# A two-layer decoder trunk on one core: last two row blocks and final norm by halves of the tokens, one mask product for two score blocks, new hand-over times

## The chip, the cores and the metric

The kernel runs on one core of a Trainium2 chip. The metric is the device time of one execution in microseconds (us); lower is better. The number for a kernel is the median over its runs.

## The reference: what is computed

Input is x, 512 tokens of 1024 features, in float32; the output has the same shape. Two layers follow each other, and a final norm ends the trunk. Each layer does:

```
hn = rms_norm(h);  p = hn @ W_in              # 1024 -> 2592, three groups of columns
yA = rwkv7(p[A])       # 4 heads of 64: a recurrence with a 64 x 64 state per head, then group norm and gate
yB = retention(p[B])   # 4 heads of 64: decaying linear attention in chunks of 128, then norm and gate
yC = latent_attention(p[C])  # 8 heads: scores of 96 features, causal softmax, values of 64
h  = h + concat(yA, yB, yC) @ W_out
h  = h + (silu(g) * u) @ W_down,  g, u = rms_norm(h) @ W_gate_up    # 1024 -> 2 x 2816 -> 1024
```

and in the end `out = rms_norm(h)`, with a learned factor per feature (`final_norm`). In the causal softmax a block of 128 queries, number ib = 0 to 3, sees (ib + 1) x 128 keys, and the last 128 of these are masked above the diagonal.

## The kernel before, in words

Features lie on the 128 partitions and the 512 tokens along the free axis, so h is eight tiles of 128 x 512. Wide products run with operands split into a high and a low part: `gemm` (L492) makes for each 128 x 128 weight tile three products, high x high, high x low and low x high. All products go through `mm` (L241, the instruction is L243) and all transposes through `tr` (L249); both pin the order of TensorE to the order of the program text. The other engines' order is chosen by the tile framework, unless an instruction is pinned in the same way.

Weights come from HBM in blocks. `fetch` loads one (L387), `convert` (L397 on) forms the high part on ScalarE (L403) and the low part by a subtraction (L404) on VectorE, or on POOL if the block's number stands in `POOL_LO`. `wnext` hands out the next block and keeps three ahead. A layer has 102 blocks: 0 to 10 time mixing and retention, 11 to 13 values, 14 to 20 gate and latents, 21 and 22 keys and values, 23 rotary queries, 24 and 25 queries, 26 to 33 the output product, then the feed-forward. The second layer's numbers begin at 102.

The order of the work is made by a small driver when the program is written out. One generator, `dense` (L1050 on), issues the wide products; others issue the time mixing (`rwkv`, `chain`, `group_norm`), the retention (`retnet`), the attention (`head`, `attend`), the key rotation and the sums of the feed-forward stage. The driver has a clock that advances by the estimated TensorE time of each product. A generator that hands over gives a delay from the table `T` (us, one dictionary per layer) or a condition; the driver then takes the generator that is due and stands first in priority (`p_...` of the same table; `dense` has 9, the last). So `T` sets where on TensorE each small piece stands between wide products. `EN` names the engine (d VectorE, p POOL, a ScalarE) of single instructions: key e542 multiplies two 128 x 512 tiles in `rwkv` (L660), key e757 adds two in `group_norm` (L881); both are on POOL. Each occurs twice in a layer.

`head` (L956 on) works one attention head. For ib = 3, 2, 1, 0 it takes a score tile in PSUM, multiplies queries and keys, adds the mask by a product of the identity with a table of 0 and -1e30, takes the row maximum on VectorE (L970), the exponential with its sum on ScalarE (L972), the reciprocal (L974) and the scaling (L975; POOL for ib = 2). The probabilities are then transposed, and `attend` multiplies them with the values when both heads of a pair are there. The query tiles are written by L1281 from a product and the factor of a norm, and the inverse roots of norms take two VectorE steps (L340, L341) with two operands in SBUF. The output product of a layer starts when the group norm's and the retention's four tiles (`mix` 0 to 3) are there; the last one hands over with the delay `group_norm3` before its last step.

In the feed-forward stage most gate and up products run over 256 tokens at a time, through sums of weight quarters and token halves (many of them on tiles of PSUM pool pd), and the down products between them over 512 (pool pm). The last step of a layer is eight row blocks of the remaining down product, each six weight tiles by three products of 512 columns; each block is added to h (L1418). In the second layer the square of a block is summed over blocks (L326, L327), and the block is scaled by `final_norm` (L1424). After the eighth block its square (L1428), a product with ones that sums over partitions (tile pm from acc and r), the inverse root by halves of the tokens (L1439 to L1443), eight products (L1446) and eight output DMAs on two queues (L1447) follow.

## Time and profile before

| | us |
|---|---|
| median of 3 runs | 1319.48 |
| lowest and highest | 1317.63, 1320.84 |
| the profiled execution, its own time | 1318.88 |
| its span, first to last instruction | 1317.1 |

The span is what a trace shows; the time also holds what lies around it, here 1.8 us. The profiled execution is 0.6 us faster than the median. In rows of the trace, PE is TensorE's products and PEld its weight loads, DVE is VectorE, ACT ScalarE, POOL GpSimd, SP the queue of the sync engine. Products are pipelined: the length of one overlaps the start of the next, so the cost of a product in a stream is the distance between starts. A product of float32 operands that is not split appears as two instructions.

### The profile page before, as it was taken

The numbers are of one execution on the slowest core, as the hardware profiler recorded it, in microseconds if no ns is written. First come the engines' busy times: TensorE is split into PE (matmuls) and PEld (weight loads), VectorE is DVE, ScalarE is ACT, GpSimd is POOL, SyncE is SP. The second block draws the span as 40 slices with busy tenths as digits, with TensorE's granted clock in tenths as the row PEclk, the third lists the DMA queues.
The fourth block names the chain that finished last, engine by engine and source line by source line (L and its number), as shares of the span: only waits on it lengthen the run. The fifth ranks groups of instructions, "written<-read, shape, count | busy, mean of one in ns | idle before, by whom it ended". The sixth has DMA issues, their size and how long they took to land. (4 is left out here: it accounts for less than half of the span.)

```text
span 1317.1 us, 20150 instructions
## 1 busy us (share of the span) xinstructions
PE 1274.7 (97%) x7774; PEld 1092.8 (83%) x7774; DVE 987.9 (75%) x1665; ACT 679.0 (52%) x1267; POOL 93.0 (7%) x82
## 2 busy tenths in 40 slices
PE   7999999899999999999999999989999999999996
PEld 5778787578899999999877887856888999999994
DVE  7797877747997777777667697686579877777774
ACT  7834456726454444545475345465355544444453
POOL 1130012200000000000012300121000000000000
PEclk9899999899999999999999899979999999999998
DMA  7434422223233333333522423131232333222231
GB/s 247 135 99 135 99 63 67 81 65 112 77 102 110 96 97 102 108 97 105 184 88 84 120 89 85 44 101 60 86 97 79 113 100 109 97 97 97 86 107 64
DMA packets 67512, 131.11 MB, mean 100 GB/s; under 512 B 29172, under 2 KB 33940, under 8 KB 67416
## 3 DMA queue, kind: packets, MB, share of 16 engines
q1 hardware_dynamic: 66040, 128.20, 31.4%
q8 instruction: 61, 1.00, 0.3%
q10 hardware_dynamic: 1232, 1.09, 0.2%
q0 software_dynamic: 144, 0.52, 0.1%
q14 instruction: 35, 0.29, 0.1%
HBM read 117.47 MB, written 9.18 MB: 96 GB/s over the span
## 5 line engine op out<-in xcount | busy, mean ns | idle before, releaser
L243 PE MATMUL pd<-u,wh 128*128 128x256 f32 (+1 forms) x3112 | 755.8, 335 | 8.4 <-ACT wh L403 5.9
L243 PEld LDWEIGHTS pd<-u,wh 128*128 128x128 f32 x3112 | 528.3, 191 | 71.6 <-issue 7.4
L243 PE MATMUL pd<-u,wl 128*128 128x256 f32 (+1 forms) x1556 | 516.9, 332 | 0.6 <-DVE wl L422 0.5
L243 PEld LDWEIGHTS pd<-u,wl 128*128 128x128 f32 x1556 | 296.9, 191 | 29.5 <-POOL wl L404 0.9
L243 PE MATMUL pm<-u,wh 128*128 128x512 f32 (+1 forms) x800 | 212.0, 352 | 0.0
L403 ACT CAST wh<-wr 128x1024 fp32r<-128x1024 f32 (+3 forms) x102 | 98.9, 974 | 167.8 <-PE pd L243 105.2
L243 PEld LDWEIGHTS pm<-u,wh 128*128 128x128 f32 x800 | 139.0, 190 | 18.3 <-DVE u L298 0.3
L404 DVE TENSOR_TENSOR wl<-wr,wh 128x1024 fp32r<-128x1024 f32 (+3 forms) x93 | 109.2, 1177 | 45.2 <-ACT wh L403 44.8
L243 PE MATMUL pm<-u,wl 128*128 128x512 f32 (+1 forms) x400 | 140.4, 351 | 0.0
L421 ACT CAST wh<-r 128x512 fp32r<-128x512 f32 x144 | 87.3, 618 | 98.9 <-PE pm L243 51.4
L421 ACT CAST wh<-wr 128x512 fp32r<-128x512 f32 x108 | 67.0, 620 | 78.6 <-PE pm L243 54.3
L422 DVE TENSOR_TENSOR wl<-r,wh 128x512 fp32r<-128x512 f32 x144 | 97.6, 687 | 8.7 <-ACT wh L421 6.5
L422 DVE TENSOR_TENSOR wl<-wr,wh 128x512 fp32r<-128x512 f32 x108 | 74.3, 689 | 24.4 <-ACT wh L421 22.3
L243 PEld LDWEIGHTS pm<-u,wl 128*128 128x128 f32 x400 | 75.7, 189 | 10.1
L1377 DVE TENSOR_TENSOR u<-u,pm 128x512 f32<-128x512 f32 x64 | 43.8, 684 | 43.9 <-PE pm L243 43.9
L243 PE MATMUL pm<-u,u 32*32 32x32 f32 (+4 forms) x728 | 68.4, 280 | 5.3 <-DVE u L742 4.0
L243 PEld LDWEIGHTS pm<-u,u 32*32 32x32 f32 (+3 forms) x728 | 51.9, 159 | 21.5 <-issue 14.0
L403 ACT CAST wh<-gg 128x1024 fp32r<-128x1024 f32 x32 | 33.6, 1049 | 42.0 <-issue 27.7
L243 PE MATMUL pd<-u,u 96*128 96x512 f32 (+3 forms) x128 | 50.9, 507 | 3.9 <-DVE u L1281 2.9
L404 POOL TENSOR_TENSOR wl<-wr,wh 128x1024 fp32r<-128x1024 f32 (+2 forms) x9 | 18.9, 2100 | 491.4 <-ACT wh L403 491.4
L432 DVE TENSOR_TENSOR r<-r,wr 128x512 f32<-128x512 f32 x72 | 49.5, 687 | 0.6
L404 DVE TENSOR_TENSOR wl<-gg,wh 128x1024 fp32r<-128x1024 f32 x32 | 39.1, 1222 | 7.9 <-ACT wh L403 7.8
(271 smaller groups left out, 1581.7 us busy)
## 6 DMA issues: line engine op xcount, KB each, us to landing
wr<-in_wts_dram SPq DMA_DIRECT2D x142, 512.0 KB, 3.5
gg<-in_wts_dram SPq DMA_DIRECT2D x32, 512.0 KB, 3.3
wr<-in_wts_dram SPq DMA_DIRECT2D x22, 384.0 KB, 3.1
u<-in_xT_dram SPq DMA_DIRECT2D x7, 512.0 KB, 7.4
tb<-tab_d SPq DMA_DIRECT2D x8, 256.0 KB, 4.2
r<-r SPq DMA_DIRECT2D x32, 64.0 KB, 2.0
h_d<-u SPq DMA_DIRECT2D x4, 512.0 KB, 3.0
u<-h_d SPq DMA_DIRECT2D x4, 512.0 KB, 4.1
```

Source lines behind the costliest of these rows:

```text
L243: tc.keep_in_program_order(nc.tensor.matmul(o, lhsT, rhs, start=start, stop=stop, skip_group_check=True))
L403: act.copy(hi[:, z], t[:, z])
L404: (pool if on in POOL_LO else dve).tensor_tensor(lo[:, z], t[:, z], hi[:, z].bitcast(F32), ALU.subtract)
L421: act.copy(hi[:, z], t)
L422: dve.tensor_tensor(lo[:, z], t, hi[:, z].bitcast(F32), ALU.subtract)
L432: E(key).tensor_tensor(o, x, y, ALU.add)
L1377: dve.tensor_tensor(hk(m), hk(m), ps, ALU.add)
```

## The change

Four things are changed.

1. The table `T` has new delays and priorities throughout, among them, in the second layer: `p_rwkv` 1.52 to 0, `p_head` 0 to 3.43, `p_gn` 0 to 2.27, `p_att` 4.43 to 0, `group_norm3` 16.24 to 19.85, `head1` 6.46 to 5.26, `head2` 0 to 0.12, `head4` 0 to 0.73; in the first: `p_rwkv` 4.24 to 7.42, `p_head` 7.77 to 8.88, `p_tab` 1.43 to 0, `head1` 6.87 to 9.39, `head3` 2.35 to 5.1, `group_norm1` 4.84 to 5.69, `group_norm2` 3.89 to 3.14, `group_norm3` 3.47 to 4.4.
2. Keys e542 and e757 go from POOL to VectorE; the low parts of weight blocks 23, 127, 129, 132 and 134 go from VectorE to POOL.
3. In `head` the blocks ib = 1 and 0 share one score tile and one mask product over 256 columns; their reciprocals are one instruction. The mask table is stored twice side by side. A head hands over three times with `head2` instead of four.
4. The last two row blocks of the second layer are done as four half blocks of 256 tokens, in the order block 6 and block 7 for the first half, block 6 for the second half, the first half's sum over partitions and inverse root, block 7 for the second half; then the first half's output, the second half's inverse root and output. Here also VectorE's instructions are pinned to the program's order.

```diff
 T, EN: as told above; new keys 'x0': 'd', 'x1': 'd', 'x2': 'p', 'x3': 'd'
+    def times(key, o, x, f):
+        if EN[key] == "a":
+            act.activation(o, x, AF.Identity, scale=f)
+        else:
+            {"d": dve, "p": pool}[EN[key]].tensor_scalar(o, x, f, None, ALU.mult)
...
-POOL_LO = (0, 21, 26, 32, 35, 106, 115, 137)
+POOL_LO = (0, 21, 23, 26, 32, 35, 106, 115, 127, 129, 132, 134, 137)
...
-CMB = np.where(np.arange(P)[None, :] <= np.arange(P)[:, None], 0.0, -1e30).astype(ml_dtypes.bfloat16)
+CMB = np.tile(np.where(np.arange(P)[None, :] <= np.arange(P)[:, None], 0.0, -1e30), 2).astype(ml_dtypes.bfloat16)
...
         q_, k_ = st["qa"][b][:, par, :], st["ka"][b][:, par, :]
         pa, pb = ur([P, 1024]), r2()
         pp = [pa[:, 896:1024], pb[:, 0:256], pa[:, 512:896], pa[:, 0:512]]
-        for ib in (3, 2, 1, 0):
-            w = (ib + 1) * P
-            ps = psd()
-            mm(ps[:, 0:w], q_[:, ib * P : (ib + 1) * P], k_[:, 0:w], True, False)
-            mm(ps[:, ib * P : w], idb, cmb, False, True)
-            nmx = sm((P, 1), tag="nmx", bufs=4)
-            dve.tensor_reduce(nmx, ps[:, 0:w], AX.X, ALU.max, negate=True)
-            ssum = sm((P, 1), tag="ssum", bufs=4)
-            act.activation(pp[ib], ps[:, 0:w], AF.Exp, bias=nmx, accum_out=ssum)
-            rs = sm((P, 1), tag="rs", bufs=4)
-            dve.reciprocal(rs, ssum)
-            (pool if ib == 2 else dve).tensor_scalar(pp[ib], pp[ib], rs, None, ALU.mult)
+
+        for ibs in ((3,), (2,), (1, 0)):
+            ps, o, at = psd(), 0, {}
+            for ib in ibs:
+                at[ib] = ps[:, o : o + (ib + 1) * P]
+                mm(at[ib], q_[:, ib * P : (ib + 1) * P], k_[:, 0 : (ib + 1) * P], ib == ibs[0], False)
+                o += (ib + 1) * P
+            n = len(ibs)
+            d0 = ibs[0] * P
+            mm(ps[:, d0 : d0 + n * P], idb, cmb[:, 0 : n * P], False, True)
+            nmx, ssum, rs = (sm((P, 2), tag=t, bufs=4) for t in ("nmx", "ssum", "rs"))
+            for i, ib in enumerate(ibs):
+                dve.tensor_reduce(nmx[:, i : i + 1], at[ib], AX.X, ALU.max, negate=True)
+            for i, ib in enumerate(ibs):
+                act.activation(pp[ib], at[ib], AF.Exp, bias=nmx[:, i : i + 1], accum_out=ssum[:, i : i + 1])
+            dve.reciprocal(rs[:, 0:n], ssum[:, 0:n])
+            for i, ib in enumerate(ibs):
+                times(f"x{ib}", pp[ib], pp[ib], rs[:, i : i + 1])
             yield T[l]["head2"]
         yield T[l]["head3"]
         ta, tb = ur([P, 1024]), r2()
...
             z = yield from last_part(late)
             finish(z, hb)
             acc, xg = None, []
-            for m in range(KT):
+            for m in range(KT if l + 1 < L else KT - 2):
                 ps = psd()
                 yield from gemm(ps, wnext(), hb, [(k, k) for k in range(nk)])
                 dve.tensor_tensor(hk(m), hk(m), ps, ALU.add)
+                acc, pr = norm_feed(hk(m), col("attn_norm", l + 1, m) if l + 1 < L else None, acc)
                 if l + 1 < L:
-                    acc, pr = norm_feed(hk(m), col("attn_norm", l + 1, m), acc)
                     xg.append(pr)
-                elif m < KT - 1:
-                    acc, _ = norm_feed(hk(m), None, acc)
+                else:
                     act.activation(hk(m), hk(m), AF.Identity, scale=col("final_norm", 0, m))
-                else:
-                    act.activation(warm, acc[:, 0:1], AF.Abs_reciprocal_sqrt)
-                    q = r2()
-                    act.activation(q, hk(m), AF.Square)
                 if l + 1 < L and m % 2 == 1:
                     sp.dma_start(h_d[:, m - 1 : m + 1, :], h_[m // 2])
 
-        act.activation(hk(m), hk(m), AF.Identity, scale=col("final_norm", 0, m))
-        ps = psm()
-        for i, t in enumerate((acc, q)):
-            mm(ps, c("ones").broadcast_to([P, P]), t, i == 0, i == 1)
-        x, y, z = r2(), r2(), r2()
-        for i in range(2):
+        act.activation(warm, acc[:, 0:1], AF.Abs_reciprocal_sqrt)
+        ws, keep = [wnext(), wnext()], tc.keep_in_program_order
+        x, y, z, q = r2(), r2(), r2(), (r2(), r2())
+
+        def block(i, j):
+            m, tk, ps = KT - 2 + j, slice(i * 256, i * 256 + 256), psd()[:, 0:256]
+            xs = [tuple(t[:, tk] for t in pr) for pr in hb]
+            yield from gemm(ps, ws[j], xs, [(k, k) for k in range(nk)])
+            keep(dve.tensor_tensor(hk(m)[:, tk], hk(m)[:, tk], ps, ALU.add))
+            act.activation(q[j][:, tk], hk(m)[:, tk], AF.Square)
+
+        def inverse(i):
+            tk, ps = slice(i * 256, i * 256 + 256), psm()[:, 0:256]
+            for j, t in enumerate((acc, *q)):
+                mm(ps, c("ones").broadcast_to([P, P]), t[:, tk], j == 0, j == 2)
+            act.activation(y[:, tk], ps, AF.Abs_reciprocal_sqrt, bias=epst[:, 0:1], scale=1.0 / D)
+            act.activation(z[:, tk], y[:, tk], AF.Square)
+            act.activation(x[:, tk], ps, AF.Identity, bias=epst[:, 0:1], scale=1.0 / D)
+            for m in (KT - 2, KT - 1):
+                act.activation(hk(m)[:, tk], hk(m)[:, tk], AF.Identity, scale=col("final_norm", 0, m))
+            keep(dve.scalar_tensor_tensor(z[:, tk], z[:, tk], -0.5, x[:, tk], ALU.mult, ALU.mult))
+            keep(dve.scalar_tensor_tensor(y[:, tk], z[:, tk], 1.5, y[:, tk], ALU.add, ALU.mult))
+
+        def give(i, ks):
             tk = slice(i * 256, i * 256 + 256)
-            act.activation(x[:, tk], ps[:, tk], AF.Identity, bias=epst[:, 0:1], scale=1.0 / D)
-            act.activation(y[:, tk], x[:, tk], AF.Abs_reciprocal_sqrt)
-            act.activation(z[:, tk], y[:, tk], AF.Square)
-            dve.scalar_tensor_tensor(z[:, tk], z[:, tk], -0.5, x[:, tk], ALU.mult, ALU.mult)
-            dve.scalar_tensor_tensor(y[:, tk], z[:, tk], 1.5, y[:, tk], ALU.add, ALU.mult)
-            for k in range(0, KT, 2):
+            for k in ks:
                 o = r2().rearrange("p (a t) -> p a t", a=2)
-                dve.tensor_tensor(o, h_[k // 2][:, :, tk], y[:, tk].unsqueeze(1).broadcast_to([P, 2, 256]), ALU.mult)
+                keep(dve.tensor_tensor(o, h_[k // 2][:, :, tk], y[:, tk].unsqueeze(1).broadcast_to([P, 2, 256]), ALU.mult))
                 (sp if k % 4 == 0 else act).dma_start(out[:, k : k + 2, tk], o)
+
+        yield from block(0, 0)
+        yield from block(0, 1)
+        yield from block(1, 0)
+        inverse(0)
+        yield from block(1, 1)
+        give(0, (0, 2, 4, 6))
+        inverse(1)
+        give(1, range(0, KT, 2))
 
     drv.spawn(9, dense())
     drv.run()
```

## Rows read from the trace of the kernel before

**Rows 1.** Part 1 of the page: busy time, share of the span and instruction count of each engine (PE is TensorE, PEld its weight loads, DVE VectorE, ACT ScalarE, POOL GpSimd), on one line.

```profile
PE 1274.7 (97%) x7774; PEld 1092.8 (83%) x7774; DVE 987.9 (75%) x1665; ACT 679.0 (52%) x1267; POOL 93.0 (7%) x82
```

**Rows 2.** Busy time by stretch. Columns: the stretch (us from the span's start), its length, busy time and instruction count of PE, PEld (weight loads), DVE, ACT and POOL, the granted TensorE clock as a share of full speed (1.00 is 2.4 GHz, 0.50 is 1.2 GHz), the share of the DMA engines' time, GB/s. The stretches are the mixing stage of layer 1 of 2, its feed-forward stage, the same two of the second layer, and what follows the last wide product.

```profile
20.00:263.00 243.00, 232.78 (x1420) 185.29 (x1419) 192.46 (x387) 143.15 (x294) 39.68 (x33) 0.97 0.34 103
263.00:640.00 377.00, 376.52 (x2380) 341.00 (x2380) 288.46 (x429) 182.73 (x320) 4.79 (x2) 1.00 0.33 100
640.00:912.00 272.00, 261.62 (x1519) 205.87 (x1518) 197.51 (x391) 148.78 (x302) 42.33 (x36) 0.96 0.32 93
912.00:1284.00 372.00, 371.57 (x2346) 337.80 (x2347) 283.04 (x418) 178.93 (x312) 2.42 (x1) 1.00 0.29 95
...
1302.40:1317.10 14.70, 1.99 (x5) 0.33 (x3) 6.94 (x13) 3.41 (x8) 0.00 (x0) 0.71 0.41 143
```

**Rows 3.** The same view, for three of the five stretches inside the mixing stages in which the granted clock stood at its lower level.

```profile
240.20:247.10 6.90, 4.97 (x16) 3.38 (x17) 5.22 (x9) 6.25 (x12) 1.26 (x1) 0.51 0.01 2
...
731.80:738.60 6.80, 6.18 (x37) 5.39 (x38) 5.63 (x9) 0.00 (x0) 6.63 (x9) 0.50 0.47 121
868.30:882.00 13.70, 13.29 (x36) 7.91 (x37) 9.70 (x32) 7.42 (x26) 3.73 (x3) 0.50 0.22 77
```

**Rows 4.** Timeline of PE in the second layer's mixing stage, the three pieces with a wait before them. Columns: start, length, engine, line, operation, out<-in, shapes, count, and in brackets the idle time before the piece and what released it.

```profile
865.14 0.67 PE L243 MATMUL pd<-u,u 96*128 96x256 f32 x2 [1.60 <-DVE u L1281]
...
867.16 0.46 PE L243 MATMUL pd<-u,u 96*128 96x128 f32 x2 [1.29 <-DVE u L1281]
...
868.71 2.08 PE L243 MATMUL pd<-u,u 96*128 96x512 f32 x2 [1.03 <-ACT u L972]
```

**Rows 5.** Timeline of DVE just before and during those waits (columns as above).

```profile
859.33 1.23 DVE L404 TENSOR_TENSOR wl<-wr,wh 128x1024 fp32r<-128x1024 f32 x1
860.47 0.69 DVE L340 SCALAR_TENSOR_TENSOR r<-r,r 128x512 f32<-128x512 f32 x1
...
863.59 0.67 DVE L341 SCALAR_TENSOR_TENSOR r<-r,r 128x512 f32<-128x512 f32 x1
```

**Rows 6.** Timeline of all engines from the end of the last wide product on (columns as above; xN merges N instructions of one kind).

```profile
1302.24 1.02 PE L243 MATMUL pm<-acc,C 128*128 128x512 f32 x2
1302.44 0.69 DVE L1418 TENSOR_TENSOR u<-u,pd 128x512 f32<-128x512 f32 x1 [2.00 <-PE pd L243]
1303.16 0.63 ACT L1428 ACTIVATE r<-u 128x512 f32<-128x512 f32 x1 [1.17 <-DVE u L1418]
...
1303.84 1.13 PE L243 MATMUL pm<-r,C 128*128 128x512 f32 x2 [0.58 <-ACT r L1428]
1305.01 0.84 ACT L1439 ACTIVATE r<-pm,epst 128x256 f32<-128x256 f32 x2 [0.46 <-PE pm L243]
1305.73 0.72 ACT L1440 ACTIVATE r<-r 128x256 f32<-128x256 f32 x2
1306.35 0.72 ACT L1441 ACTIVATE r<-r 128x256 f32<-128x256 f32 x2
1306.79 0.76 DVE L1442 SCALAR_TENSOR_TENSOR r<-r,r 128x256 f32<-128x256 f32 x2 [3.66 <-ACT r L1441]
1307.47 0.75 DVE L1443 SCALAR_TENSOR_TENSOR r<-r,r 128x256 f32<-128x256 f32 x2
1308.14 4.90 DVE L1446 TENSOR_TENSOR r<-u,r 128x512 f32<-128x512 f32 x8
...
1309.45 3.99 ACTq L1447 DMA_DIRECT2D out_dram<-r  x4
```

**Rows 7.** The chain of waits in the feed-forward stage: start, length, engine, tile, line, count. The pieces on tile pd are products over 256 columns, those on tile pm over 512.

```profile
1020.80 4.32 PE pd L243 x36
1025.12 5.47 PE pm L243 x24
```

**Rows 8.** Timeline of PE in a score stage: a short score block (two instructions), its mask product, and the next block.

```profile
210.03 0.39 PE L243 MATMUL pd<-u,u 96*128 96x128 f32 x2
210.25 0.22 PE L243 MATMUL pd<-cmb,idb 128*128 128x128 bf16 x1
210.31 0.86 PE L243 MATMUL pd<-u,u 96*128 96x384 f32 x2
```

**Rows 9.** Groups of instructions by line and shape: busy us, mean ns of one, idle time before them with its releaser. First DVE: low parts of weights (L404), the reciprocals of the attention heads (L974) and one product of the time mixing (L653, the shape of keys e542 and e757). Then POOL: low parts of weights, and the line of key e757 (L881).

```profile
L404 DVE TENSOR_TENSOR wl<-wr,wh 128x1024 fp32r<-128x1024 f32 x64 | 80.8, 1266 | 40.6 <-ACT wh L403 40.2 <-issue 0.2
...
L974 DVE RECIPROCAL rs<-ssum 128x1 f32<-128x1 f32 x64 | 9.4, 156 | 3.5 <-ACT u L972 1.9 <-ACT r L972 1.4
...
L653 DVE TENSOR_TENSOR u<-u,r 128x512 f32<-128x512 f32 x4 | 2.7, 681 | 0.0
...
L404 POOL TENSOR_TENSOR wl<-wr,wh 128x1024 fp32r<-128x1024 f32 x6 | 14.9, 2491 | 486.4 <-ACT wh L403 486.4
...
L881 POOL TENSOR_TENSOR r<-r,u 128x512 f32<-128x512 f32 x4 | 5.1, 1267 | 19.9 <-ACT r L880 19.9
```

**Rows 10.** Timeline of DVE and POOL: two equal products with two operands in SBUF (L722), the second beside a subtraction on POOL.

```profile
727.06 0.75 DVE L722 SCALAR_TENSOR_TENSOR r<-u,PC,u 128x512 f32<-128x512 f32 x1
...
728.65 1.28 POOL L307 TENSOR_TENSOR r<-r,r 128x512 fp32r<-128x512 f32 x1 [6.78 <-issue]
728.70 1.78 DVE L722 SCALAR_TENSOR_TENSOR r<-u,PC,u 128x512 f32<-128x512 f32 x1
```

**Rows 11.** One line's instructions, the output DMAs issued on the ScalarE queue: duration in ns min/median/max, first and last start in us.

```profile
L1447 ACTq DMA_DIRECT2D out_dram<-r x4: 378/379/396, 1309.5 to 1313.1; - x4
```

More of the change, by code (lines that the diff above doesn't have):

```diff
@@ L41 @@
-EN = {'e499': 'd', 'e535': 'd', 'e541': 'd', 'e542': 'p', 'e563': 'p', 'e564': 'p', 'e565': 'd', 'e592': 'd', 'e593': 'd', 'e594': 'd', 'e595': 'd', 'e757': 'p', 'e759': 'd', 'e773': 'p', 'e826': 'd', 'e968': 'p', 'e969': 'd', 'e970': 'd', 'e909': 'd', 'e1037': 'd', 'e1090': 'd', 'e1096': 'p', 'e1097': 'd', 'e1171': 'd', 'e302': 'd', 'e273': 'd', 'c511': 'a', 'c639': 'a', 'c646': 'a', 'c647': 'a', 'c686': 'a', 'c716': 'a', 'c736': 'a', 'c1008': 'a', 'c498': 'd', 'h1': 'd', 'h2': 'd', 'h3': 'p', 'h4': 'p', 'h5': 'd', 'h6': 'd', 's1': 'd', 's2': 'd', 's3': 'd', 's4': 'd', 'z': 'd'}
+T = [{'tables1': 0, 'norm1': 0, 'p_rwkv': 7.42, 'p_ret': 0.1, 'p_head': 8.88, 'p_tab': 0, 'p_gn': 0.03, 'p_att': 0.0, 'p_kr': 0, 'angles1': 0, 'angles2': 2.63, 'angles3': 1.74, 'angles4': 0, 'angles5': 0, 'rwkv1': 4.34, 'rwkv2': 8.45, 'rwkv3': 0, 'rwkv4': 0, 'rwkv5': 0.0, 'rwkv6': 1.03, 'rwkv7': 0.0, 'rwkv8': 0.34, 'rwkv9': 4.2, 'rwkv10': 3.21, 'rwkv11': 0.76, 'rwkv12': 4.16, 'rwkv13': 2.42, 'rwkv14': 0.0, 'rwkv15': 0.91, 'rwkv16': 0.36, 'rwkv17': 0.74, 'rwkv18': 14.19, 'rwkv19': 2.06, 'rwkv20': 0, 'rwkv21': 0.0, 'chain1': 0.9, 'chain2': 2.38, 'chain3': 0.55, 'group_norm1': 5.69, 'group_norm2': 3.14, 'group_norm3': 4.4, 'retnet1': 5.58, 'retnet2': 0, 'retnet3': 0.74, 'retnet4': 4.98, 'retnet5': 3.23, 'retnet6': 0.0, 'head1': 9.39, 'head2': 0.76, 'head3': 5.1, 'head4': 1.71, 'attend1': 1.77, 'key_rope1': 1.87, 'latent_norm1': 6.26, 'latent_norm2': 3.58, 'latent_norm3': 0.33, 'sums1': 0.0, 'sums2': 3.84, 'sums3': 5.51, 'sums4': 7.06, 'sums5': 5.22, 'sums6': 5.16, 'sums7': 2.65},
+     {'norm1': 0, 'p_rwkv': 0, 'p_ret': 5.86, 'p_head': 3.43, 'p_gn': 2.27, 'p_att': 0, 'p_kr': 2.33, 'rwkv1': 3.59, 'rwkv2': 5.03, 'rwkv3': 0, 'rwkv4': 0, 'rwkv5': 0, 'rwkv6': 3.29, 'rwkv7': 0.0, 'rwkv8': 7.7, 'rwkv9': 1.93, 'rwkv10': 2.94, 'rwkv11': 0.8, 'rwkv12': 3.89, 'rwkv13': 0.02, 'rwkv14': 0, 'rwkv15': 0.43, 'rwkv16': 0.0, 'rwkv17': 0.73, 'rwkv18': 13.88, 'rwkv19': 0, 'rwkv20': 0.42, 'rwkv21': 0, 'chain1': 0.28, 'chain2': 0.96, 'chain3': 0.67, 'group_norm1': 4.53, 'group_norm2': 2.33, 'group_norm3': 19.85, 'retnet1': 2.13, 'retnet2': 4.42, 'retnet3': 0, 'retnet4': 2.48, 'retnet5': 0, 'retnet6': 0.0, 'head1': 5.26, 'head2': 0.12, 'head3': 8.59, 'head4': 0.73, 'attend1': 0, 'key_rope1': 1.53, 'latent_norm1': 3.38, 'latent_norm2': 0.7, 'latent_norm3': 0.52, 'sums1': 2.53, 'sums2': 2.41, 'sums3': 11.53, 'sums4': 0.22, 'sums5': 0, 'sums6': 11.24, 'sums7': 0.72}]
@@ new lines @@
+EN = {'e499': 'd', 'e535': 'd', 'e541': 'd', 'e542': 'd', 'e563': 'p', 'e564': 'p', 'e565': 'd', 'e592': 'd', 'e593': 'd', 'e594': 'd', 'e595': 'd', 'e757': 'd', 'e759': 'd', 'e773': 'p', 'e826': 'd', 'e968': 'p', 'e969': 'd', 'e970': 'd', 'e909': 'd', 'e1037': 'd', 'e1090': 'd', 'e1096': 'p', 'e1097': 'd', 'e1171': 'd', 'e302': 'd', 'e273': 'd', 'c511': 'a', 'c639': 'a', 'c646': 'a', 'c647': 'a', 'c686': 'a', 'c716': 'a', 'c736': 'a', 'c1008': 'a', 'c498': 'd', 'h1': 'd', 'h2': 'd', 'h3': 'p', 'h4': 'p', 'h5': 'd', 'h6': 'd', 's1': 'd', 's2': 'd', 's3': 'd', 's4': 'd', 'z': 'd', 'x0': 'd', 'x1': 'd', 'x2': 'p', 'x3': 'd'}
@@ L519, in tile_trunk @@
     idb = cst.tile([P, P], BF16, tag="idb", name="idb")
-    cmb = cst.tile([P, P], BF16, tag="cmb", name="cmb")
+    cmb = cst.tile([P, 2 * P], BF16, tag="cmb", name="cmb")
     ctk = cst.tile([P, 64], F32, tag="ctk", name="ctk")
```

2 lines of the change are left out of this document (removed).

## The prediction

> **What bounds the kernel now.** I read the shares of busy time first: TensorE is busy 97% of the span, VectorE 75%, ScalarE 52% [rows 1]. So a change pays only where it shortens TensorE's own work, fills a time in which TensorE waits, or shortens what follows its last product. Next the busy time by stretch [rows 2]: both feed-forward stages have under 0.5 us of idle TensorE, and nothing in them is touched but the last two row blocks. The mixing stages leave 243.0 - 232.8 = 10.2 and 272.0 - 261.6 = 10.4 us idle, and after the last wide product TensorE works 2.0 of 14.7 us. Third, the granted clock: three stretches in the mixing stages stand at the lower level, 1.2 GHz (0.50 or 0.51), the longest 13.7 us with 13.3 us of TensorE busy [rows 3]. It comes behind three waits of 1.60, 1.29 and 1.03 us, two of them for VectorE [rows 4]. So there are three pools: the tail of 14.7 us, some 21 us of waits, and the lower clock.
>
> **The tail, the surest term.** Before, the last wide product ends at about 1302.4; then come an addition, a square, the sum over partitions of that square, two halves of the inverse root, eight products of 0.61 us (4.90 / 8) and their DMAs [rows 6]. After the change the last two row blocks are done as four half blocks. A product over 256 columns costs 4.32 / 36 = 0.120 us, one over 512 costs 5.47 / 24 = 0.228 [rows 7], so four half blocks of 18 take 8.64 us against 8.21. They start where the last two blocks start now, 1302.4 - 8.2 = 1294.2. The last weight block is wanted a half block, 2.2 us, earlier than now; weights are converted three blocks ahead in the code, so this costs nothing; if that cover were missing, TensorE would wait at most those 2.2 us. Three half blocks end at 1300.7. Three sums over the partitions of 256 columns follow; one over 512 is 1.02 us [rows 6], so three halves cost at most 1.5, and I take 1.35: 1302.05. The fourth half block ends at 1304.2. That is 1.8 us later than now, but the first half's inverse is ready by then: ScalarE needs 1.2 us for three steps (0.84, 0.72 and 0.72 for two each), VectorE 0.7 for two (0.76 and 0.75 for four in all) [rows 6].
>
> From 1304.2 I walk both engines. VectorE: the addition over 256 columns, 0.4, to 1304.6; four products of the first half, 2.45, to 1307.05; two steps of the second inverse, 0.7, to 1307.75; four products, 2.45, to 1310.2. The other chain: square, 0.4 (half shape of L1440, 0.72 / 2, and a hand-over), to 1305.1; the last sum, half of the 1.17 us from 1303.84 to 1305.01 and some latency, to 1305.75; three ScalarE steps to 1306.9. That is before VectorE comes free at 1307.05, so VectorE sets the end: 1310.2 against 1308.14 + 4.90 = 1313.04 now [rows 6]. **Minus 2.85 us.** The DMA behind the last product stays. Bounds: if the first half's four products cost nothing, the end is 1306.9 + 0.7 + 2.45 = 1310.05, minus 3.0. If ScalarE's queue holds the second inverse behind the first half's output DMAs, whose issue waits for VectorE's fourth product (1307.05) and takes 0.38 [rows 11], the end is 1307.45 + 1.15 + 0.7 + 2.45 = 1311.75, minus 1.3. I take the walk, since nothing forces that order.
>
> **One mask for the two short score blocks.** Per head two masks of 128 columns become one of 256, one weight load, one score tile and one reciprocal go. On TensorE a mask takes 0.06 us from its start at 210.25 to the next start at 210.31 [rows 8]. A product of 256 columns costs 0.120 [rows 7], which is two masks: then nothing is gained, one end. If the wider mask costs no more than a narrow one, 16 heads save 16 x 0.06 = 1.0, the other end. I take the middle, **minus 0.5**. The 16 reciprocals, 2.5 us at 0.156 [rows 9], come off VectorE, but the first exponential of the pair may now wait for both maxima: hidden, while other heads are in flight; if not, it is part of the next term.
>
> **Engines and hand-over times, one term.** Five low parts of weights (three of 1024 columns, two of 768) move from VectorE (1.27 at most) to POOL (2.49), eight products of 512 columns move the other way (0.68 on VectorE, 1.27 on POOL) [rows 9]: VectorE gets at most 6.3 less and 5.4 more, so the totals nearly cancel, and POOL at 7% has room [rows 1]. No DMA moves with them, except that the order of weight loads follows the order of work. What counts is the place. Just before the three waits VectorE forms a low part at 859.33, 1.23 us [rows 5]. By the order of the conversions I take it for that of weight block 129, one of the five; moved to POOL it lets the products that TensorE waits for start earlier. Against it, e757 twice adds 0.68 on VectorE in the same stretch and must wait there for a ScalarE step. In the second layer the heads' start comes 1.2 us earlier (head1 6.46 to 5.26), before the last query products have run out, and the steps head2 and head4 get a delay above 0, so that the output product can come between heads once its inputs stand; the group norm's last step comes 3.6 us later and works the other way. Where several tasks are due there, the time mixing now goes ahead of the heads. All other times shift the places of the waits in ways that no row shows. Bounds from the nearest rows, the place in [rows 3, 4]: if it goes, 3.9 us of waits and half of 13.3 us are saved, minus 10.5; if another such place opens, plus 10.5. I take **minus 1.6**, the first wait of that place [rows 4], since its cause is VectorE's queue, which is relieved just ahead of it; the rest I count as a draw.
>
> One row speaks against these moves: a VectorE product with two operands in SBUF took 0.75 us alone, and 1.78 when a POOL subtraction of 1.28 us had started 0.05 before it [rows 10]; it waited out nearly all of that subtraction. The Trainium skill, page "SBUF — State Buffer", section "SBUF: two separate sides", has this as a rule: a VectorE instruction with two SBUF inputs and a GpSimd instruction that reads SBUF share one pair of ports, and whoever starts first holds it for its whole length. By that rule, with which the row agrees, each moved low part could hold VectorE for up to 2.49 us instead of freeing it for 1.27, and the five would add some 6 us to VectorE's queue net of what they take off, not remove 6.
>
> **Sum.** 2.85 + 0.5 + 1.6 = 4.95. The profiled execution took 1318.88 us (span 1317.1), so 1313.9; the median of the runs, 1319.48, lies 0.6 above, so I forecast 1314.5. A measurement of this kernel can tell about 0.2%, 2.6 us, from no change; the tail alone is just that.
>
> **Rivals.** *The bad place goes:* the waits of [rows 4] and the lower clock behind them vanish: 1319.5 - 3.35 - 10.5 = 1305.6. For it: the edits aim at VectorE's load there. Against it: heads alone still fill that stretch until the group norm is through. Chance 0.20. *The tail gives little:* ScalarE's queue order leaves 1.3 us, the mask nothing, the rest a draw: 1318.2, no difference to measure. Chance 0.18; this is also the case in which the change does not do what it says, since halves that overlap nothing are only more instructions. *Slower:* at the same place POOL takes the low part at 859.33 and holds VectorE's next step, L340 with two operands in SBUF, until 861.8 instead of 860.47, 1.3 us; e757 waits there twice for a ScalarE step (0.63 [rows 6]) and takes 0.68, 2.6 more behind L341 at 863.59 [rows 5]; TensorE's waits grow by 3.9, and the lower clock lasts one more stretch like the shortest in [rows 3], 6.8 us, of which half is lost, 3.4. That is plus 7.3, and with the tail and mask 1319.5 - 3.35 + 7.3 = 1323.4. It decides as soon as waits and clock cost over 3.35. For it: [rows 10]. Against it: most of VectorE's work there reads PSUM. Chance 0.17. By the Trainium skill's rule above (page "SBUF — State Buffer") this is the case that comes.
>
> **Numbers.** Forecast 0.45, its own range 1311 to 1316.8; with the larger gain faster is 0.65, same 0.18, slower 0.17. The range 1305 to 1323 leaves out the far ends of the two outer rivals, under 0.2 together.
>
> **What would show it.** Right: sums over the partitions stand on TensorE ahead of the last half block; the first half's output products run while the second half's inverse is formed; from the end of the last wide product to the end of the span it takes 14.7 - 1.8 - 2.85 = 10.05 us instead of 14.7; three score tiles a head instead of four; the idle TensorE time of the second mixing stage falls below 10.4 us. Wrong in the tail: ScalarE steps of the second inverse behind an output DMA, or VectorE idle between the two halves' products. Wrong in the rest: the lower clock lasts longer than the 27.4 us of [rows 3] in these places, or TensorE waits over 3.9 us at the heads of the second layer; then the hand-over term, the least founded of the three, has failed.

## The result and the profile after

The median went from 1318.77 us (6 runs, 1317.12 to 1322.65) to **1309.92 us** (6 runs, 1308.13 to 1313.48): ratio 0.9931 [0.9912, 0.9951]. That is 8.9 us less by the medians and 9.1 by the ratio; 9.0 stands for it below. The forecast was 1314.5 with the range 1305 to 1323. The profiled execution of after took 1308.13 us, the fastest of its six; its lines carry numbers 7 higher than before up to about L1000 and 13 higher from there on. (In the text, mm is L250 instead of L243, the low parts are L411 instead of L404, and so on; in e4 and e10 all lines are 7 higher.) Medians and ratios below leave out one run that fell far out, one of the twelve of e9: 1578.8 us at a granted clock of 0.747.

First the shares of busy time, as [rows 1]:

```profile
PE 1266.3 (97%) x7802; PEld 1088.7 (83%) x7802; DVE 982.6 (75%) x1653; ACT 680.7 (52%) x1271; POOL 91.8 (7%) x79
```

TensorE issues 28 instructions more than before, and is busy 1274.7 - 1266.3 = 8.4 us less. Its idle time falls only from 1317.1 - 1274.7 = 42.4 to 1306.3 - 1266.3 = 40.0 us. So of the 10.8 us between the two profiled executions, 2.4 is idle time and 8.4 is less busy time, for the same work and those 28 instructions. It goes with a higher clock: the mean granted clock was 0.983 before and 0.993 after. Of the six runs of after, this one has the highest clock (their median is 0.989), so the medians differ by less than this pair.

Next the stages, as [rows 2] (stretch, length, busy time and count of PE, PEld, DVE, ACT, POOL, granted clock, DMA share, GB/s), the last one from the addition of the last wide product to the end:

```profile
20.00:257.00 237.00, 227.87 (x1413) 182.23 (x1411) 192.44 (x384) 143.19 (x293) 35.47 (x30) 1.00 0.36 106
257.00:634.00 377.00, 376.03 (x2380) 340.35 (x2377) 286.83 (x427) 182.59 (x322) 5.25 (x3) 1.00 0.32 100
634.00:903.00 269.00, 257.99 (x1498) 204.35 (x1498) 195.93 (x375) 144.81 (x288) 38.52 (x33) 0.97 0.33 97
903.00:1275.00 372.00, 370.62 (x2364) 335.28 (x2359) 281.80 (x427) 183.22 (x326) 8.85 (x5) 1.00 0.28 94
1295.40:1306.30 10.90, 1.51 (x6) 0.67 (x4) 6.16 (x12) 2.29 (x5) 0.00 (x0) 0.75 0.55 192
```

The first mixing stage leaves 9.1 us idle (before 10.2), the second 11.0 (before 10.4). What changed in them is the clock: 0.97 to 1.00 in the first, 0.96 to 0.97 in the second. Ahead of the tail, five stretches with 37.5 us stood at the lower level before (three of them in [rows 3]); after, three with 13.6 us, in this execution none in the first layer:

```profile
727.50:730.90 3.40, 3.40 (x23) 2.89 (x22) 3.30 (x5) 0.00 (x0) 3.23 (x6) 0.50 0.54 135
799.20:802.60 3.40, 3.08 (x11) 2.51 (x11) 0.98 (x3) 2.00 (x5) 0.00 (x0) 0.50 0.02 5
860.60:867.40 6.80, 6.33 (x15) 3.85 (x16) 4.40 (x14) 3.88 (x15) 2.46 (x2) 0.50 0.23 77
```

The place in the second layer that the prediction wanted cleared [rows 4] still has its waits, with another releaser:

```profile
854.83 1.10 PE L250 MATMUL pd<-u,u 96*128 96x512 f32 x2 [0.81 <-PE pd L250]
861.07 1.65 PE L250 MATMUL pd<-u,u 96*128 96x384 f32 x2 [3.35 <-ACT u L985]
```

That is 4.16 us against the 3.9 of [rows 4], and 6.8 us at the lower clock behind it instead of 13.7. The low part that the prediction wanted off VectorE there [rows 5] did go, to POOL:

```profile
851.02 2.42 POOL L411 TENSOR_TENSOR wl<-wr,wh 128x1024 fp32r<-128x1024 f32 x1 [4.46 <-ACT wh L410]
```

So taking it off VectorE did not do away with the waits.

The tail, all engines, as [rows 6] (start, length, engine, line, operation, out<-in, shapes, count, and in brackets the idle time before it and its releaser; ACTq is a DMA issued on ScalarE's queue):

```profile
1292.18 1.02 PE L250 MATMUL pm<-r,C 128*128 128x256 f32 x4
...
1295.39 0.42 DVE L1448 TENSOR_TENSOR u<-u,pd 128x256 f32<-128x256 f32 x1
...
1295.72 2.49 DVE L1467 TENSOR_TENSOR r<-u,r 128x512 f32<-128x512 f32 x4
...
1297.05 0.47 ACT L1455 ACTIVATE r<-pm,epst 128x256 f32<-128x256 f32 x1 [0.25 <-PE pm L250]
1297.05 0.39 ACTq L1468 DMA_DIRECT2D out_dram<-r  x1
...
1298.25 0.38 ACTq L1468 DMA_DIRECT2D out_dram<-r  x1
1298.67 0.47 ACT L1457 ACTIVATE r<-pm,epst 128x256 f32<-128x256 f32 x1 [0.70 <-DVE r L1467]
1299.18 0.42 DVE L1460 SCALAR_TENSOR_TENSOR r<-r,r 128x256 f32<-128x256 f32 x1 [0.96 <-ACT r L1457]
...
1300.16 2.50 DVE L1467 TENSOR_TENSOR r<-u,r 128x512 f32<-128x512 f32 x4
```

The first half's products (from 1295.72) run while the second half's inverse is formed, as forecast. But ScalarE's third step (L1457) waits 0.70 us behind the output DMA at 1298.25, which itself waits for a product of the first half; VectorE then stands idle for 0.96 us. From the start of block 5's addition to the end of the span it takes 22.8 us before (1294.28 to 1317.1) and 20.8 after (1285.48 to 1306.3): **minus 2.0**.

### The profile page after: what moved, and what is told of

Read it like the earlier page. It is cut to its first block, busy times and chain, and to the rows that moved or that the text cites. A ratio compares the mean times of both kernels' runs of the same rounds, so it can differ in the third digit from the quotient of the medians.

```text
span 1306.3 us, 20183 instructions
## 1 busy us (share of the span) xinstructions
PE 1266.3 (97%) x7802; PEld 1088.7 (83%) x7802; DVE 982.6 (75%) x1653; ACT 680.7 (52%) x1271; POOL 91.8 (7%) x79
## 4 chain that ended last, share of the span: by engine, by line
PE 88%; DVE 6%; ACT 3%; DMA 1%; issue 1%; SPq 0%; DVEq 0%; ACTq 0%
PE pd L250 61%; PE pm L250 25%; PE pm L257 2%; DMA wr<-in_wts_dram 1%; DMA u<-in_xT_dram 1%; DVE wl L411 0%; DVE r L729 0%; DVE r L1467 0%; DVE u L1034 0%; ACT wh L410 0%; DVE r L348 0%; DVE u L1024 0%; DVE u L723 0%; DVE u L719 0%; DVE u L1245 0%
## 5 line engine op out<-in xcount | busy, mean ns | idle before, releaser
L250 PE MATMUL pd<-u,wh 128*128 128x256 f32 (+1 forms) x3136 | 757.1, 334 | 10.7 <-ACT wh L410 5.8
L250 PEld LDWEIGHTS pd<-u,wh 128*128 128x128 f32 x3136 | 529.8, 191 | 73.5 <-issue 8.7
L250 PE MATMUL pd<-u,wl 128*128 128x256 f32 (+1 forms) x1568 | 518.6, 331 | 0.7 <-DVE wl L429 0.6
L250 PEld LDWEIGHTS pd<-u,wl 128*128 128x128 f32 x1568 | 298.7, 191 | 29.4 <-POOL wl L411 0.9
L250 PE MATMUL pm<-u,wh 128*128 128x512 f32 (+1 forms) x800 | 212.0, 352 | 0.7 <-DVE u L1034 0.7
L250 PEld LDWEIGHTS pm<-u,wh 128*128 128x128 f32 x800 | 139.1, 190 | 18.8 <-DVE u L1034 0.9
L250 PE MATMUL pm<-u,wl 128*128 128x512 f32 (+1 forms) x400 | 140.3, 351 | 0.0
L411 DVE TENSOR_TENSOR wl<-wr,wh 128x1024 fp32r<-128x1024 f32 (+3 forms) x88 | 102.6, 1170 | 41.0 <-ACT wh L410 40.7
L250 PEld LDWEIGHTS pm<-u,wl 128*128 128x128 f32 x400 | 75.7, 189 | 10.3
L250 PE MATMUL pm<-u,u 32*32 32x32 f32 (+4 forms) x728 | 67.4, 277 | 4.9 <-DVE u L749 2.8
L411 POOL TENSOR_TENSOR wl<-wr,wh 128x1024 fp32r<-128x1024 f32 (+3 forms) x14 | 29.7, 2125 | 594.1 <-ACT wh L410 594.1
L250 PEld LDWEIGHTS pm<-u,u 32*32 32x32 f32 (+3 forms) x728 | 50.4, 157 | 21.9 <-issue 14.5
L410 ACT CAST wh<-gg 128x1024 fp32r<-128x1024 f32 x32 | 33.6, 1050 | 41.5 <-issue 27.4
L250 PE MATMUL pd<-u,u 96*128 96x128 f32 (+3 forms) x128 | 45.1, 465 | 4.2 <-ACT u L985 3.4
L411 DVE TENSOR_TENSOR wl<-gg,wh 128x1024 fp32r<-128x1024 f32 x32 | 39.1, 1222 | 7.7 <-ACT wh L410 7.7
```

Source lines behind the costliest of these rows:

```text
L250: tc.keep_in_program_order(nc.tensor.matmul(o, lhsT, rhs, start=start, stop=stop, skip_group_check=True))
L410: act.copy(hi[:, z], t[:, z])
L411: (pool if on in POOL_LO else dve).tensor_tensor(lo[:, z], t[:, z], hi[:, z].bitcast(F32), ALU.subtract)
```

## The experiments

Each kernel ran 6 or 12 times. The number of a run's experiment is in its name; times are medians in us, ratios are to the kernel before on the same chip, and the clock is the median over the runs of a kernel (before 0.981 or 0.983, after 0.989).

| run | median | before | ratio [95%] | clock |
|---|---|---|---|---|
| e1_tail | 1316.62 | 1319.35 | 0.9983 [0.9968, 0.9997] | 0.983 |
| e2_mask | 1320.31 | 1319.35 | 0.9995 [0.9977, 1.0012] | 0.983 |
| e3_times | 1332.25 | 1319.35 | 1.0097 [1.0076, 1.0118] | 0.979 |
| e4_engines | 1323.14 | 1319.35 | 1.0019 [1.0004, 1.0035] | 0.980 |
| e5_old_times | 1318.74 | 1319.96 | 0.9988 [0.9970, 1.0007] | 0.983 |
| e6_old_times_1 | 1321.76 | 1319.96 | 1.0006 [0.9990, 1.0022] | 0.984 |
| e7_old_times_2 | 1307.54 | 1319.96 | 0.9906 [0.9885, 0.9927] | 0.988 |
| e8_out_sp | 1307.65 | 1319.96 | 0.9909 [0.9887, 0.9931] | 0.990 |
| e9_times_mask | 1320.89 | 1319.90 | 1.0009 [0.9994, 1.0023] | 0.983 |
| e10_times_engines | 1319.48 | 1319.90 | 1.0008 [0.9992, 1.0024] | 0.985 |
| e11_only_23 | 1318.74 | 1318.87 | 0.9997 [0.9985, 1.0010] | 0.985 |
| e12_both | 1305.13 | 1318.87 | 0.9901 [0.9881, 0.9921] | 0.990 |

**Each part alone.** To the kernel before, e1 adds only the half blocks of the tail, e2 only the shared mask with its doubled table, e3 only the whole new table of times, e4 only the engine moves; each diff is the one of the change, here cut to its first lines.

```diff
-            for m in range(KT):
+            for m in range(KT if l + 1 < L else KT - 2):
...
+        yield from block(0, 0)
...
```

> The kernel before with only the last two row blocks and the norm done by halves. Theory A (three separate gains: tail, mask, order): 2.0 us faster, ratio 0.9985, since the traces show 22.8 us from the start of the addition of block 5 to the end of the span before, 20.8 after; the rest of the trace as before. Theory B (the tail as I walked it in the prediction): 2.85 us, ratio 0.9978. Theory C (the gain is all order and clock): under 1 us.

```diff
-        for ib in (3, 2, 1, 0):
+        for ibs in ((3,), (2,), (1, 0)):
...
```

> The kernel before with only the shared mask product. A head hands over three times instead of four, so the order on TensorE moves too. Theory A: 0.5 us faster, ratio 0.9996, within 0.2% of before. Theory B (fewer score tiles relieve the score stage): 2 to 4 us faster and the waits at the heads of the second layer shorter than 3.9 us. Theory C (the shared tile makes both exponentials wait): slower by 1 to 3 us.

```diff
-'p_rwkv': 4.24, 'p_head': 7.77, 'p_tab': 1.43
+'p_rwkv': 7.42, 'p_head': 8.88, 'p_tab': 0
...
```

> The kernel before with only the new table of hand-over times and priorities. Theory A: this carries most of what the tail doesn't, 5 to 7 us faster, ratio 0.995 to 0.996, with the lower clock shorter than before's 37.6 us. Theory B (the times fit only the engines and the mask they came with): within 2.6 us of before or slower. Theory C (the moved engines carry the gain): within 2 us.

```diff
-'e542': 'p', 'e757': 'p'
+'e542': 'd', 'e757': 'd'
-POOL_LO = (0, 21, 26, 32, 35, 106, 115, 137)
+POOL_LO = (0, 21, 23, 26, 32, 35, 106, 115, 127, 129, 132, 134, 137)
```

> The kernel before with only the five low parts on POOL and e542 and e757 on VectorE. Theory A: a draw, within 2.6 us of before. Theory B (VectorE relieved ahead of the waits of the second layer): 3 to 6 us faster and the wait of 1.6 us for L1281 gone. Theory C (POOL holds the shared ports, the slower rival of the prediction): 2 to 5 us slower, two-operand products on VectorE stretched beside the moved low parts.

The differences here are the ratios times the time before. The tail by itself gives 0.17%, 2.2 us, near the 2.0 read from the traces. The mask by itself cannot be told from nothing (-0.7 us, -3.0 to +1.6). The engine moves alone cost 2.5 us, and the times alone 12.8. The four do not add up: -2.2 - 0.7 + 2.5 + 12.8 = +12.4, where all together give -9.0. So the gain beside the tail is a joint one, and the times are in it: without them, tail, mask and engines nearly add up (-2.2 - 0.7 + 2.5 = -0.4, and e5 below has -1.6, -4.0 to +0.9). e4 also tests the slower rival at its place. TensorE in the second layer, the waits before the heads:

```profile
870.93 0.46 PE L250 MATMUL pd<-u,u 96*128 96x128 f32 x2 [2.98 <-DVE u L1288]
873.05 2.07 PE L250 MATMUL pd<-u,u 96*128 96x512 f32 x2 [1.61 <-ACT u L979]
```

They sum to 4.59 us, somewhat over the 3.92 of [rows 4]. VectorE and POOL there:

```profile
861.93 2.41 POOL L411 TENSOR_TENSOR wl<-wr,wh 128x1024 fp32r<-128x1024 f32 x1 [4.46 <-ACT wh L410]
863.58 0.68 DVE L1288 TENSOR_TENSOR u<-pd,fB 64x512 f32<-64x512 f32 x1 [0.39 <-PE pd L250]
864.19 0.70 DVE L347 SCALAR_TENSOR_TENSOR r<-r,r 128x512 f32<-128x512 f32 x1
```

The low part runs on POOL from 861.93 to 864.34. In that time VectorE works at L1288, which reads PSUM, at its usual 0.68, and the inverse root step (L347) starts only 0.15 us before the low part ends and takes 0.70, as in [rows 5]. So POOL holds nothing up at that place, and the waits are there although the low part left VectorE. The sign of the slower rival holds for this part alone, its mechanism at that place does not. Elsewhere in e4 one product does stretch beside a moved low part (L334, 1.93 us at 156.63), but the moves end other such stretches: VectorE's products of 512 columns beside an instruction on POOL lose 5.9 us in all (counted over 0.69 us, for those longer than 0.9), and lost 9.0 before. What costs e4 its 2.5 us is not shown.

**Which layer's times.** e5 is the changed kernel with the old table (both edits below), e6 with the old table of the first layer only (the first edit), e7 of the second only (the second edit).

```diff
-'p_rwkv': 7.42, 'p_head': 8.88, 'p_tab': 0
+'p_rwkv': 4.24, 'p_head': 7.77, 'p_tab': 1.43
...
-'p_rwkv': 0, 'p_head': 3.43
+'p_rwkv': 1.52, 'p_head': 0
...
```

> The changed kernel with the old table of hand-over times (halves, mask and engines stay). Theory A: loses what the times carry, so 2.5 to 4 us faster than before, ratio 0.997 to 0.998. Theory B (times and engines only work together): 2 us faster, the tail alone. Theory C (engines carry the gain): 8 to 9 us faster, like the changed kernel.

> The changed kernel with the old times in the first layer only. In the traces the first layer's mixing stage gives 5.5 to 6 us of the gain, at equal wide products. Theory A (the times do it): 3 to 4 us faster than before instead of 9. Theory B (the engines or the mask do it there): still 8 to 9 us faster.

> The changed kernel with the old times in the second layer only, where the traces show 3 us of the gain. Theory A: 6 us faster than before instead of 9, the output product again behind all heads. Theory B (moving the output product between the heads is what counts): 3 us faster or less, since the lower clock comes back at the heads. Theory C: still 9 us faster.

With the first layer's old times the gain is gone (e6, 1321.76; e5, 1318.74). With the second layer's old times it is all there (e7, 1307.54, 0.94% [0.73, 1.15]; the changed kernel 0.69% [0.49, 0.88]). So what the new times bring lies in the **first** layer; those of the second bring nothing that can be measured. Both pairs that differ in them alone, e6 and e5, the changed kernel and e7, stand on the side of a loss, by the ratios 2.4 and 3.3 us, neither of them clear of the noise.

**The outputs' queue.** e8 is the changed kernel with all output DMAs on SP's queue.

```diff
-                (sp if k % 4 == 0 else act).dma_start(out[:, k : k + 2, tk], o)
+                sp.dma_start(out[:, k : k + 2, tk], o)
```

> The changed kernel with all output DMAs on the sync engine's queue, so that none stands in ScalarE's queue. In the changed kernel's trace one ScalarE step of the second inverse (L1457) starts at 1298.67, behind an output DMA that waited for the fourth product of the first half, and VectorE then idles 0.96 us. Theory A (that queue costs the part of the tail I missed): 0.8 to 1 us faster than the changed kernel, ratio to before 0.7 thousandths lower. Theory B (the sync queue then issues eight DMAs at 0.38 us each in a row and lands later): equal or slower.

The median is 2.3 us below that of the changed kernel, but the two intervals overlap. The traces show the piece itself, from the last addition (L1448) to the first of the second half's products (L1467). VectorE in e8:

```profile
1299.25 0.42 DVE L1448 TENSOR_TENSOR u<-u,pd 128x256 f32<-128x256 f32 x1
...
1303.08 2.50 DVE L1467 TENSOR_TENSOR r<-u,r 128x512 f32<-128x512 f32 x4
```

That is 3.83 us, against 1300.16 - 1295.39 = 4.77 in the changed kernel: 0.94 less. From the last addition to the end of the span it is 10.05 (1299.25 to 1309.3), just what the prediction forecast for the whole piece.

**Which partner the times need.** e9 is the kernel before with times and mask, e10 with times and engine moves. Their edits are those of e3 with those of e2 or e4. e11 is the changed kernel where of the engine moves only the low part of block 23 is left:

```diff
-'e542': 'd', 'e757': 'd'
+'e542': 'p', 'e757': 'p'
-POOL_LO = (0, 21, 23, 26, 32, 35, 106, 115, 127, 129, 132, 134, 137)
+POOL_LO = (0, 21, 23, 26, 32, 35, 106, 115, 137)
```

> The kernel before with the new times and the shared mask, old engines, old tail. The new times alone made it 12.8 us slower, with mask, engines and tail together 9 us faster; in the traces the two part in the first layer between the start of its heads and its feed-forward stage. Theory M (the times were fitted to three hand-overs a head, so the mask is the partner): 5 to 7 us faster than before, mean granted clock 0.988 or more. Theory E (the engines are the partner, low part 23 and e757 among them): still over 8 us slower, clock 0.98. Theory ME (both are needed): within 3 us of before.

> The kernel before with the new times and the new engines, four masks a head, old tail. Theory M: still over 8 us slower, clock 0.98. Theory E: 5 to 7 us faster, clock 0.988 or more. Theory ME: within 3 us of before.

> The changed kernel with only one of the seven engine moves left: the low part of block 23 on POOL; e542 and e757 back on POOL, low parts 127, 129, 132 and 134 back on VectorE. In the traces the times without this move wait 2.99 and 3.44 us at about 160 and 177 us in the first layer, with a lower clock behind them; with all engine moves these are 1.71 and 0.47 and the clock stays up. Theory 23 (that one low part, 153.44 on VectorE, changes the order of VectorE's queue there, and is the part of the engines that the times need): 7 to 10 us faster than before, clock 0.988 or more. Theory G (it is e757 or the other moves): 1 to 3 us faster, the tail alone.

Each partner takes off most of the 12.8 us that the times alone cost (by the ratios, e9 stands at +1.2 and e10 at +1.0 us, neither to be told from nothing), and only both lead below the time before. e11, which is times, mask and tail with block 23's low part, gives nothing either, so the rest of the engine moves is needed. The traces show two places in the first layer's mixing, one for each partner.

*Place 1.* TensorE from 156 to 178 us, first in e11, then in the changed kernel:

```profile
160.19 1.22 PE L250 MATMUL pd<-u,wh 128*128 128x512 f32 x2 [2.99 <-DVE u L339]
177.24 0.98 PE L250 MATMUL pm<-R,u 128*128 128x128 f32 x3 [3.43 <-DVE R L855]
```

```profile
158.59 0.73 PE L250 MATMUL pd<-u,wh 128*128 128x512 f32 x2 [1.71 <-DVE u L339]
168.75 0.68 PE L250 MATMUL pm<-R,u 128*128 128x128 f32 x4 [0.47 <-DVE R L855]
```

The first product is 1.6 us later in e11, the second, which needs the time mixing's tile R, 8.5 us. VectorE there, e11 first:

```profile
167.00 0.69 DVE L1220 SCALAR_TENSOR_TENSOR r<-pm,rB 128x512 f32<-128x512 f32 x1 [3.47 <-PE pm L250]
...
170.32 0.96 DVE L411 TENSOR_TENSOR wl<-wr,wh 128x768 fp32r<-128x768 f32 x1
...
176.80 0.49 DVE L855 TENSOR_TENSOR R<-pm,EX 128x128 f32<-128x128 f32 x2
```

```profile
165.09 0.69 DVE L1220 SCALAR_TENSOR_TENSOR r<-pm,rB 128x512 f32<-128x512 f32 x1
...
168.31 0.49 DVE L855 TENSOR_TENSOR R<-pm,EX 128x128 f32<-128x128 f32 x2
...
172.94 0.95 DVE L411 TENSOR_TENSOR wl<-wr,wh 128x768 fp32r<-128x768 f32 x1
```

In e11 VectorE stands idle for 3.47 us at L1220, waiting for TensorE; its later work is queued behind that, among it a low part (170.32), and R (176.80) behind the low part. TensorE in turn waits 3.43 us for R. In the changed kernel R stands ahead of the low part. The first wait is longer in e11 for a like reason: e11 and then the changed kernel,

```profile
157.22 0.69 DVE L935 TENSOR_TENSOR r<-pm,C 128x512 f32<-128x512 f32 x1 [1.12 <-PE pm L250]
...
159.39 1.40 DVE L339 SCALAR_TENSOR_TENSOR u<-pd,PC,u 128x512 fp32r<-128x512 f32 x2
```

```profile
157.79 1.41 DVE L339 SCALAR_TENSOR_TENSOR u<-pd,PC,u 128x512 fp32r<-128x512 f32 x2 [1.50 <-ACT u L338]
...
160.66 0.69 DVE L935 TENSOR_TENSOR r<-pm,C 128x512 f32<-128x512 f32 x1
```

TensorE waits for L339, and in e11 L935 stands ahead of it in VectorE's queue. The clock of two stretches, 155 to 185 and 230 to 260 us, in e11 and then in the changed kernel (columns as in [rows 2]):

```profile
155.00:185.00 30.00, 23.58 (x223) 17.86 (x222) 20.07 (x32) 13.90 (x27) 0.55 (x1) 0.72 0.34 86
230.00:260.00 30.00, 25.55 (x146) 16.62 (x145) 22.21 (x58) 27.23 (x66) 10.49 (x8) 1.00 0.09 33
```

```profile
155.00:185.00 30.00, 27.51 (x289) 22.32 (x288) 25.48 (x45) 18.22 (x39) 0.14 (x1) 1.00 0.36 97
230.00:260.00 30.00, 25.90 (x143) 17.33 (x142) 23.48 (x57) 23.18 (x53) 3.73 (x3) 1.00 0.30 106
```

Behind the waits, e11 has 0.72 at place 1 where the changed kernel keeps 1.00, and issues 223 products instead of 289 in the same 30 us. Waits and clock read alike in e3 and e9 (2.99 with 3.44 or 3.56 us, clock 0.72 and 0.77), and in e10 and e12 as in the changed kernel (1.71 with 0.48 or 0.47, clock 1.00). So the engine moves decide place 1, and block 23 is not the one: e11 and e9 stand alike. In the traces of e11 and the changed kernel TensorE's 7802 products have the same order; VectorE's order first differs at e542 (L667), at about 62 us. The moved e757 comes only at about 240 us. That leaves e542 as the likely one; it was not run alone. At its own place e542 on POOL also holds VectorE up, in e11:

```profile
61.41 1.60 POOL L667 TENSOR_TENSOR u<-u,u 128x512 f32<-128x512 f32 x1 [12.43 <-DVE u L660]
61.77 1.78 DVE L666 TENSOR_TENSOR u<-u,r 128x512 f32<-128x512 f32 x1
```

L666 takes 0.68 us at 61.45 in the changed kernel, and e542 on VectorE another 0.68 at 62.65, together less than the 1.78. How that leads to the other order 100 us later is not shown; the tile framework chooses it when the program is written out.

*Place 2.* TensorE from 230 to 242 us, e10 (four masks) and then the changed kernel (shared mask):

```profile
235.65 0.48 PE L257 MATMUL pm<-ident,u 128*128 128x128 f32 x1 [3.18 <-ACT r L885]
```

```profile
234.73 0.44 PE L257 MATMUL pm<-ident,u 128*128 128x128 f32 x2 [1.19 <-ACT r L885]
235.01 0.82 PE L250 MATMUL pd<-u,u 96*128 96x256 f32 x4
235.66 0.27 PE L250 MATMUL pd<-cmb,idb 128*128 128x256 bf16 x1
235.78 1.02 PE L250 MATMUL pd<-u,u 96*128 96x512 f32 x2
...
237.91 0.33 PE L257 MATMUL pm<-ident,u 128*128 128x128 f32 x1 [1.05 <-ACT r L885]
```

With four masks a head, one wait of 3.18 us for the group norm (e3 has it too, 3.18), and a clock of 0.89 over 230 to 260 us in both. With the shared mask, score blocks stand between the two waits for the same step, no wait is over 1.5 us, and the clock stays at 1.00 (in e8, e9, e11 and e12 too; in e7, with the same waits of 1.20 and 1.05 us, it is 0.94). What the mask edit brings at this place is another order of TensorE's work, since a head hands over three times instead of four; which line of that edit does it was not taken apart. The product itself saves nothing: two narrow ones take 0.12 us by [rows 8], the wide one 235.78 - 235.66 = 0.12.

The two places add up. At the 1,111th product with weights, in the first layer's feed-forward stage, e3 stands at 376.7 us, e10 at 365.4, e9 at 368.2, e12 at 358.0: engine moves 11.3 us, mask 8.5, both 18.7. Before stands at 364.4: the new times alone lose 12.3, and the two partners take off more than that.

**Both better versions at once.** e12 is the changed kernel with e7's table and e8's queue.

```diff
-'p_rwkv': 0, 'p_head': 3.43
+'p_rwkv': 1.52, 'p_head': 0
...
-                (sp if k % 4 == 0 else act).dma_start(out[:, k : k + 2, tk], o)
+                sp.dma_start(out[:, k : k + 2, tk], o)
```

> The changed kernel with the old times in the second layer and all output DMAs on the sync queue. Theory A (the two gains add): 12 to 14 us faster than before, ratio 0.990 or less, median below 1308. Theory B (the second layer's times and the queue gave only what the clock happened to give in those runs): 9 to 12 us faster, no better than either alone.

e12 has the lowest median, 1305.13 us, ratio 0.9901 [0.9881, 0.9921]; its interval overlaps those of e7 and e8, so whether their two gains add is not settled. Its tail, ScalarE and VectorE:

```profile
1294.78 0.47 ACT L1455 ACTIVATE r<-pm,epst 128x256 f32<-128x256 f32 x1 [0.25 <-PE pm L250]
1295.15 0.47 ACT L1457 ACTIVATE r<-pm,epst 128x256 f32<-128x256 f32 x1
1295.51 0.41 ACT L1456 ACTIVATE r<-r 128x256 f32<-128x256 f32 x1
...
1296.95 2.50 DVE L1467 TENSOR_TENSOR r<-u,r 128x512 f32<-128x512 f32 x4
```

The three ScalarE steps follow each other, and the second half's products start 3.49 us after the first half's (1293.46 to 1296.95), where the changed kernel needs 4.44 (1295.72 to 1300.16).

## Why the prediction was right in sign and short in size

**The tail** was forecast at -2.85 and measured at -2.0 (trace) and -2.2 (e1). The half blocks went as worked out: from the first half-block product at 1285.28 to the addition of the last half block at 1295.39 it takes 10.11 us, against 8.64 + 1.35 = 9.99 forecast. The step that failed is the last one: I wrote that nothing forced ScalarE's queue to hold the second inverse behind the output DMAs, and in part it did. From the last addition to the end 10.9 us pass against 10.05 forecast, some 0.9 more; e8 and e12, with the output DMAs off that queue, need 10.05 and 10.08. The bound of -1.3 assumed the whole inverse behind the fourth product; only its third step stood behind the second DMA.

**The mask** was forecast at -0.5 between 0 and -1.0. Three score tiles a head are there, and the end that a wide product costs as much as two narrow ones is the right one: 0.12 us against 0.12. As a term of its own it is not measurable. Its real effect, the order at place 2, was not in the term.

**Engines and hand-over times** is the step that failed: "the place" was set in the second layer, the rest counted as "a draw", at -1.6. The term came out at about -9.0 + 2.2 + 0.7 = -6.1, inside its bounds of 10.5, from places that I had not looked at. That it has the sign I gave it is luck: the reason for the -1.6, a low part that leaves VectorE's queue ahead of the heads, came true and took no wait away (4.59 us in e4, 4.16 in the changed kernel). The second layer's waits did not go (4.16 us against 3.9, and the idle time of its mixing stage 11.0 against 10.4): two of the signs that I had named for that term, and both came out against it; only the third, the lower clock, fell as hoped, to 13.6 us in all (from 37.5 in five stretches; the prediction went by the 27.4 of three). The price of e542 was off too: I counted 0.68 us more on VectorE for each, but on POOL the first of each layer had held VectorE's neighbouring product for 1.1 us (1.78 instead of 0.68 above). What the new times bring is in the first layer's mixing, where the changed order keeps the clock up, and it comes of three edits that cost time or give nothing alone. That such edits can be summed was the hidden assumption: an edit of one engine's list changes the order in which instructions queue, and with it which wait is long.

**The rivals.** *The bad place goes* named 1305.6, closer in size than the forecast, but by another place; e7, without the new times there, keeps the gain. *The tail gives little* had its mechanism in part, at some 0.9 us instead of 2.85 - 1.3 = 1.55. *Slower* fits the engine moves alone (+2.5 us, e4), not by the port: at that place L347 took 0.70, and over the whole trace less time is lost beside POOL than before. The port itself shows elsewhere in the changed kernel, VectorE and POOL at 153 us:

```profile
153.30 1.84 POOL L411 TENSOR_TENSOR wl<-wr,wh 128x768 fp32r<-128x768 f32 x1 [12.86 <-ACT wh L410]
153.75 1.94 DVE L334 TENSOR_TENSOR acc<-acc,r 128x512 f32<-128x512 f32 x1 [0.87 <-ACT r L333]
```

L334 takes 0.69 us at 1286.86 in the same kernel and 1.94 beside block 23's low part on POOL. The Trainium skill, page "SBUF — State Buffer", section "SBUF: two separate sides", says that a VectorE instruction with two SBUF inputs and a GpSimd instruction that reads SBUF share a pair of ports and exclude each other; these rows agree. The 1.25 us did not reach TensorE: in e11, which has that move, and in e9, which has not (there the low part takes VectorE 0.96 us and L334 0.68), the next product that waits starts at 160.19 and 160.22 us, behind the same wait of 2.99.

**What stays open.** Which of the engine moves place 1 needs is argued from the order of the programs, not run. Why the second layer's new times bring nothing is not explained: single profiled executions scatter too much to read it. The changed kernel and e8 differ in the output DMAs alone, yet at the 4,106th product with weights, in the second layer's feed-forward stage, they stand 4.4 us apart (995.2 and 999.7).

## What to carry to other kernels

Where one engine is busy 97% of the time, look at the busy time itself and not only at the waits: here 8.4 of the 10.8 us between the two traces were less busy time at a higher granted clock, and the waits in sum hardly moved. Edits of order, engines and hand-over times are to be measured together and in pairs, since alone they gave +12.8, +2.5 and -0.7 us, and together about -6. And a DMA that waits for data should not stand in the queue of an engine whose next step is on the path to the end: 0.94 us here.
